# Depthwise convolution in the first mixer: taps behind the bonus products, one tile of channels on ScalarE and GpSimd, the other on VectorE

## The chip, the cores and the metric

The kernel runs on one core of a Trainium2 chip. The metric is the device time of one execution in microseconds; smaller is better. The engines of the core work in parallel, each on its own queue in the order of that queue: TensorE (PE) for matrix products, VectorE (DVE), ScalarE (ACT), GpSimd (POOL), and SyncE (SP), which issues the transfers.

## The reference, cut to what matters

Two blocks follow one another on 256 tokens of 1024 channels. The first has two layers; each is a gated feed-forward, a mixer and another feed-forward. The mixer projects the normalised input and gives its columns to three parts: a recurrence with six heads (RWKV), an attention with six heads and three dilations, and a convolution on 256 channels. The second block (one layer) isn't touched.

```python
def _conv_mixer(u, dw_w, dw_b, ln_w, ln_b):
    z = u[..., :D_CONV] * jax.nn.sigmoid(u[..., D_CONV:])        # D_CONV = 256
    z = lax.conv_general_dilated(z, dw_w[:, None, :], window_strides=(1,),
                                 padding=[(CONV_WIDTH - 1, 0)],   # CONV_WIDTH = 31
                                 dimension_numbers=('NWC', 'WIO', 'NWC'),
                                 feature_group_count=D_CONV) + dw_b
    mu = jnp.mean(z, axis=-1, keepdims=True)
    var = jnp.mean(jnp.square(z - mu), axis=-1, keepdims=True)
    z = (z - mu) * lax.rsqrt(var + CONV_LN_EPS) * ln_w + ln_b
    return jax.nn.silu(z)
...
    # first_block, layer l
    y_rwkv = _rwkv7_mixer(p_rwkv, ...)   # its last lines:
        # bonus = sum(rh * kh * r_k, axis=-1) * vh;  return (y + bonus) * g
    y_attn = _attention_mixer(...)
    y_conv = _conv_mixer(...)
    mix = jnp.concatenate([y_rwkv, y_attn, y_conv], axis=-1)
    x = x + mix @ w_out[l]
```

Each channel of the convolution is a sum of 31 products: the channel's row of 256 tokens, shifted by 0 to 30 tokens, times one weight, plus a bias.

## The kernel before

Activations lie with channels on the 128 partitions and the 256 tokens along the row. So the convolution's 256 channels are two tiles of 128x256, and a tap of one tile is one operation on 128x256 values with one weight per partition. All matrix products are in fp32 in two halves: ScalarE makes the upper half `whi` of each weight chunk `wraw` (L299), VectorE the rest `wlo` (L275), and TensorE multiplies with both.

The helpers record every operation under their own lines: L275 is `tt` (add, sub, mul), L288 `ts` (a tensor with one or two scalars), L294 `stt` (a tensor times a scalar per partition, plus or times a second tensor), L299 `act`, L302 `mm`, L306 `tr` (a transpose on TensorE). So in the profile operations are told apart by their tiles.

The tiles `Ea` and `Eb` are one scratch space, `E`, cut at element 6144: what is taken from `E` at a lower offset lies in `Ea`, the rest in `Eb`. `bigA`, `bigB` and `F` are further scratch spaces whose parts are used again for many things. The scheduler tracks waits by what overlaps there.

`mixer1` (L601 on) writes out one mixer. `project` makes the projection in pairs of tiles (`win`). `conv_in` projects the convolution's own four tiles and then, at raised priority (`first(PRI)`, PRI = 300), starts the generator `conv`: the gate `z` (in `Eb`), and the halved weights `wh` (tile `cwh`, one buffer for both layers). `rwkv` builds the recurrence's inputs, from the key norms `kks` through the bonus products `bon` (TensorE multiplies `rkb`, three tiles of r_k at `E(5632)`, with `r`). After `bon` come the triangular solves of its two streams, each with five doubling levels (`lt`, `l1` and a 32x32 transpose, L837), and then `z` and `u`. Between them it calls `taps()`, which carries the generator on over its 31 taps. Then `attn1` records the attention, whose scores get their biases from GpSimd (L288 and L275, 128x384, tile `F`) and whose maxima and sums VectorE takes (L1103, L1106), and then `mixer1` runs the end of `conv`: the mean by TensorE (`cm`), its subtraction (`Eb<-cm`), the square, the second mean, the scaling, silu, and the split for `w_out`. The first products with `w_out` (`woa`) take the convolution's two tiles, then the attention's; they fill TensorE between the recurrence's steps.

In a tap of before, ScalarE multiplies by the weight into `th` (128x256, one place per tile of channels) and GpSimd adds it to the sum `o`:

```python
for j in range(31):
    for i in range(2):
        a, w = z[:, i, j:j + TOK], wh[:, i * 31 + j:i * 31 + j + 1]
        if j == 0: self.act(o[:, i, :], a, AF.Identity, scale=w, bias=...)
        else:
            self.act(th[:, i, :], a, AF.Copy, scale=w)
            self.add(o[:, i, :], o[:, i, :], th[:, i, :], nc.gpsimd)
```

That is 62 ACTIVATEs and 60 adds in a layer. `z`, `th` and `o` all lie in `Eb`.

Each engine's order isn't that of the code. A list scheduler places the operations by priority, which falls in the order in which the code records them and is raised under `first`, and by estimated times; only what `pin` marks keeps its written order. So a call that moves, as `taps()` does, gives its operations another priority, and all four engines' orders around it are laid anew.

Of the kernel before, what the change touches and what calls it, by code (L numbers as in the profile page):

```python
# [15 lines left out]
AF = mybir.ActivationFunctionType  # L16
# [5 lines left out]
TOK = 256  # L22
# [192 lines left out]
class Ker:  # L215
# [385 lines left out]
    def mixer1(self, l, nxt):  # L601
# [57 lines left out]
        def conv_in():  # L659
            proj(10, 14)  # L660
            with self.first(PRI):
                next(conv)
        tail = self.rwkv(l, cb, col, lt, ps_sh, R1, R2, E, conv_in, lambda: next(conv))
        proj(14, len(order))
        with self.first(1000):
# [59 lines left out]
    def rwkv(self, l, cb, col, lt, ps_sh, R1, R2, E, between, taps):  # L725
        nc = self.nc
# [5 lines left out]
        th = E(5376, TOK)  # L732
# [83 lines left out]
        def stream(c_):  # L816
# [36 lines left out]
            if c_ == 0:  # L853
# [6 lines left out]
                for i in range(3):  # L860
                    ps = ring("bon")
                    self.mm(ps[:, 0:TOK], rkb[:, i, :], r[:, i, :], True, True)
                    self.mul(bv[:, i, :], ps[:, 0:TOK], v[:, i, :])
            if c_ == 0:
                taps()
            Tm = R2(3072 + c_ * 384, 384)
            for b in (2, 4, 8, 16, 32):

# [35 lines left out]
            if c_ == 0:  # L904

                for z in range(2):
                    ps = ring("bkt")
                    for i in range(3):
                        self.tr(ps[:, i * P:(i + 1) * P], BK[:, 2 * i, z, :])
                    self.act(BKt[:, z, :], ps[:, 0:384])  # L910
                for i in range(3):
                    ps = ring("lo2")
                    self.mm(ps[:, 0:TOK], lw[64:128, i * P:(i + 1) * P], th[64:128, :], True, True)

                    self.stt(bv[:, i, :], bv[:, i, :], col("rwkv_ln_b", i), ps[:, 0:TOK], ALU.add, ALU.mult)
                    self.act(g[:, i, :], ps[:, 0:TOK], AF.Copy, scale=col("rwkv_ln_w", i))

            psz = st["z", c_] = [ring("z0"), ring("z1")]
            for h in range(6):
# [12 lines left out]
        def tail(fill):  # L932
# [76 lines left out]
            gb(1, rw1, yc1)  # L1009

        stream(0)
        stream(1)
        for i in range(3):
            self.mixh[i] = (out[2 * i], out[2 * i + 1])
        return tail

    def conv(self, l, cb, col, cu, E):
        nc = self.nc
        W = 30 + TOK
        z = E(7168, 2, W)  # L1020
        nc.gpsimd.memset(z[:, :, 0:30], 0.0)
        th = E(7744, 2, TOK)
        self.act(th, cu[:, 2:4, :], AF.Tanh, scale=0.5)
        self.stt(z[:, :, 30:W], th, 1.0, cu[:, 0:2, :], ALU.add, ALU.mult)
        wh = self.t([P, 62], "cwh")
        self.ts(wh, col("conv_dw_w", 0, 62), 0.5, None)
        o = E(8256, 2, TOK)
        yield

        for j in range(31):  # L1030
            for i in range(2):
                a, w = z[:, i, j:j + TOK], wh[:, i * 31 + j:i * 31 + j + 1]
                if j == 0:
                    self.act(o[:, i, :], a, AF.Identity, scale=w, bias=col("conv_dw_b", i))
                else:
                    self.act(th[:, i, :], a, AF.Copy, scale=w)
                    self.add(o[:, i, :], o[:, i, :], th[:, i, :], nc.gpsimd)
        yield
        ps = self.pd("cm")
        for i in range(2):  # L1040
            self.mm(ps[:, 0:TOK], self.ones, o[:, i, :], i == 0, i == 1)
        for i in range(2):
            self.stt(o[:, i, :], ps[:, 0:TOK], -1.0 / 256, o[:, i, :])
        sq = E(7744, 2, TOK)
        self.act(sq, o, AF.Square)
        self.add(sq[:, 0, :], sq[:, 0, :], sq[:, 1, :])
        self.nacc = sq[:, 0, :]
        r = self.norm_cols(eps=1e-5, n=256.0, st="c", pool=self.pd)
        ps = self.pd("cb")
        for tt in range(2):  # L1050
            self.bcast_tok(ps[:, tt * P:(tt + 1) * P], r[:, tt:tt + 1])
        self.mul(o, o, ps[:, 0:TOK].unsqueeze(1).to_broadcast([P, 2, TOK]))
        for i in range(2):
            t1 = self.w1("ct1")
            self.ts(o[:, i, :], o[:, i, :], col("conv_ln_w", i), col("conv_ln_b", i))
            self.act(t1, o[:, i, :], AF.Tanh, scale=0.5)
            self.ts(t1, t1, 0.5, 0.5)
            self.mul(o[:, i, :], o[:, i, :], t1)
            self.mix_out(6 + i, o[:, i, :])
# [871 lines left out]
```

## Time and profile before

| | |
|---|---|
| median of 3 runs | 1712.67 us (1712.02 to 1713.77) |
| profiled execution | 1711.67 us |
| its span, first to last instruction | 1709.9 us |
| mean granted TensorE clock | 0.984 |
| mixer of layer 0, `kks` to `u` | 233.35 to 350.05 us |
| mixer of layer 1, `kks` to `u` | 787.28 to 895.68 us |
| TensorE, VectorE, ScalarE, GpSimd busy | 97%, 79%, 55%, 28% of the span |

The page's busy shares are means over the whole span. A mixer has other limits than the feed-forwards, so it is read by stretches. The views by window give, for a stretch, its length and each engine's busy time with the number of operations, then the granted clock of TensorE as a share of full speed and the transfers' share. The timeline gives single instructions with start and duration, and in brackets the engine's idle time just ahead of them and what ended it. Groups by form give a total and a mean in ns.

### The profile page before, as it was taken

The page shows a single profiled execution, that of the slowest core. Times are in us where ns is not written, and L with a number is a line of the kernel's source. Part 1 is how long each engine was busy: PE and PEld are TensorE (multiplying, and loading weights), DVE is VectorE, ACT ScalarE, POOL GpSimd, SP SyncE. Part 2 cuts the span into 40 slices and gives each one's busy share as a digit, 9 for nine tenths or more (in the row PEclk, how much of TensorE's full clock was granted, in tenths as well). Part 3 has the DMA queues.
Part 4 walks back from the last instruction along what each step waited for, and adds up shares of the span by engine and source line. Part 5 has one row for each costly group of instructions (what it writes and reads, how often), then busy time and mean ns, then how long its engine had stood idle before and what let it go on. Part 6 is the DMA issues. An engine that isn't in the chain of part 4 may idle for free.

```text
span 1709.9 us, 35224 instructions
## 1 busy us (share of the span) xinstructions
PE 1659.5 (97%) x14120; PEld 1567.6 (92%) x14120; DVE 1349.1 (79%) x2364; ACT 943.8 (55%) x1735; POOL 477.2 (28%) x429
## 2 busy tenths in 40 slices
PE   8999999999999999999999999999999999999997
PEld 8999997689999999999778999998988779999976
DVE  7886798568885788578967888787887867788877
ACT  5554476346454554457644555475657565566633
POOL 2221138212220122114921221063651140111142
PEclk9999998899999999999999999999999999999999
DMA  7775641027766687664102787644433226566533
GB/s 240 256 240 194 214 151 63 2 74 233 238 228 191 219 288 281 196 207 148 62 14 89 259 297 268 207 153 135 158 124 102 74 89 209 175 184 186 161 124 122
DMA packets 82132, 293.02 MB, mean 171 GB/s; under 512 B 9008, under 2 KB 10800, under 8 KB 81968
## 3 DMA queue, kind: packets, MB, share of 16 engines
q1 hardware_dynamic: 81968, 290.78, 52.0%
q8 instruction: 110, 1.80, 0.4%
q14 instruction: 54, 0.44, 0.1%
HBM read 289.69 MB, written 1.05 MB: 170 GB/s over the span
## 4 chain that ended last, share of the span: by engine, by line
PE 82%; DVE 10%; POOL 4%; ACT 2%; issue 2%; DMA 0%; SPq 0%; DVEq 0%; POOLq 0%; ACTq 0%
PE gu L302 35%; PE dn L302 17%; PE p L302 7%; PE win L302 5%; DVE wlo L275 3%; PE o L302 2%; POOL Eb L275 2%; PE woa L302 1%; DVE Eb L294 1%; PE ob L302 1%; DVE bigA L275 1%; PE s L302 1%; PE pt L306 1%; PE y L302 1%; ACT whi L299 1%
## 5 line engine op out<-in xcount | busy, mean ns | idle before, releaser
L299 ACT ACTIVATE whi<-wraw 128x1024 fp32r<-128x1024 f32 (+2 forms) x485 | 495.6, 1026 | 471.0 <-issue 132.8
L275 DVE TENSOR_TENSOR wlo<-wraw,whi 128x1024 fp32r<-128x1024 f32 (+2 forms) x477 | 574.7, 1205 | 173.7 <-ACT whi L299 170.6
L302 PE MATMUL gu<-xm,whi 128*128 128x256 f32 x2816 | 486.7, 278 | 6.1 <-ACT whi L299 4.0
L302 PEld LDWEIGHTS gu<-xm,whi 128*128 128x128 f32 x2816 | 428.1, 189 | 7.1 <-ACT whi L299 4.0
L302 PE MATMUL gu<-xm,wlo 128*128 128x256 f32 x1408 | 390.5, 278 | 2.8 <-DVE wlo L275 2.8
L302 PEld LDWEIGHTS gu<-xm,wlo 128*128 128x128 f32 x1408 | 265.4, 189 | 4.4 <-DVE wlo L275 4.3
L275 POOL TENSOR_TENSOR bigB<-Ea,bigA 128x256 fp32r<-128x256 f32 x88 | 123.5, 1406 | 421.0 <-ACT bigA L299 421.0
L302 PE MATMUL dn<-bigB,whi 128*128 128x256 f32 x704 | 194.1, 276 | 0.0
L302 PE MATMUL dn<-bigA,wlo 128*128 128x256 f32 x704 | 194.1, 276 | 0.0
L302 PE MATMUL dn<-bigA,whi 128*128 128x256 f32 x704 | 193.9, 276 | 0.0
L302 PE MATMUL p<-xm,whi 128*128 128x256 f32 x912 | 176.4, 288 | 1.9 <-DVE bigB L294 1.9
L302 PEld LDWEIGHTS p<-xm,whi 128*128 128x128 f32 x912 | 144.2, 191 | 8.4 <-issue 7.1
L302 PE MATMUL win<-xm,whi 128*128 128x256 f32 x736 | 136.1, 285 | 0.0
L302 PEld LDWEIGHTS dn<-bigB,whi 128*128 128x128 f32 x704 | 132.1, 188 | 0.0
L302 PEld LDWEIGHTS dn<-bigA,wlo 128*128 128x128 f32 x704 | 132.1, 188 | 0.0
L302 PEld LDWEIGHTS dn<-bigA,whi 128*128 128x128 f32 x704 | 132.0, 188 | 0.0
L275 POOL TENSOR_TENSOR Eb<-Eb 128x256 f32<-128x256 f32 x120 | 104.7, 900 | 96.2 <-ACT Eb L299 95.8
L302 PE MATMUL p<-xm,wlo 128*128 128x256 f32 x456 | 130.0, 285 | 0.0
L302 PE MATMUL gu<-bigA,whi 128*128 128x258 f32 x704 | 128.1, 284 | 0.0
L302 PEld LDWEIGHTS win<-xm,whi 128*128 128x128 f32 x736 | 114.4, 191 | 4.0 <-issue 4.0
L302 PEld LDWEIGHTS gu<-bigA,whi 128*128 128x128 f32 x704 | 109.7, 191 | 0.0
L302 PE MATMUL win<-xm,wlo 128*128 128x256 f32 x368 | 104.2, 284 | 0.0
(500 smaller groups left out, 3219.9 us busy)
## 6 DMA issues: line engine op xcount, KB each, us to landing
wraw<-in_wflat_dram SPq DMA_DIRECT2D x464, 512.0 KB, 3.6
Ea<-in_wmod_dram SPq DMA_DIRECT2D x24, 512.0 KB, 5.1
Eb<-in_wmod_dram SPq DMA_DIRECT2D x24, 512.0 KB, 4.6
F<-in_wflat_dram SPq DMA_DIRECT2D x22, 512.0 KB, 4.2
Ea<-in_cc_dram SPq DMA_DIRECT2D x6, 512.0 KB, 6.1
cb<-in_cb_dram SPq DMA_DIRECT2D x2, 608.0 KB, 4.7
Ea<-in_ctxT_dram SPq DMA_DIRECT2D x1, 1024.0 KB, 6.3
out_dram<-bigA SPq DMA_DIRECT2D x4, 256.0 KB, 2.2
```

Source lines behind the costliest of these rows:

```text
L275: (eng or self.nc.vector).tensor_tensor(out=out, in0=a, in1=b, op=op)
L294: self.nc.vector.scalar_tensor_tensor(out=out, in0=a, scalar=s, in1=b, op0=op0, op1=op1)
L299: self.nc.scalar.activation(out=out, in_=a, func=func, **kw)
L302: return self.nc.tensor.matmul(out, l, r, start=start, stop=stop, skip_group_check=True)
L306: self.nc.tensor.transpose(out, a, self.ident[0:n, 0:n])
```

## The change

Three things change, in both layers. `taps()` is called behind the solve of stream 0 instead of ahead of its doubling levels. The sum `o` moves from `E(8256)` to `E(5632)`, that is from `Eb` into `Ea`, onto the place of `rkb`, which the bonus products read; so no tap can be done before `bon`. And the taps of the second tile of channels (i = 1) become one VectorE operation each, 30 in a layer, multiplying and adding at once, with no ScalarE and GpSimd operation; those of the first tile stay a ScalarE product and a GpSimd add, 30 pairs in a layer, with two places for the product, used in turn. The first tap (j = 0) stays on ScalarE for both.

```diff
@@ -861,8 +861,6 @@
                     self.mul(bv[:, i, :], ps[:, 0:TOK], v[:, i, :])
-            if c_ == 0:
-                taps()
             Tm = R2(3072 + c_ * 384, 384)
             for b in (2, 4, 8, 16, 32):
@@ -914,6 +912,8 @@
                     self.act(g[:, i, :], ps[:, 0:TOK], AF.Copy, scale=col("rwkv_ln_w", i))
+            if c_ == 0:
+                taps()
 
             psz = st["z", c_] = [ring("z0"), ring("z1")]
@@ -1024,7 +1024,8 @@
-        o = E(8256, 2, TOK)
+
+        o = E(5632, 2, TOK)
         yield
@@ -1032,9 +1033,12 @@
                     self.act(o[:, i, :], a, AF.Identity, scale=w, bias=col("conv_dw_b", i))
+                elif i:
+                    self.stt(o[:, i, :], a, w, o[:, i, :])
                 else:
-                    self.act(th[:, i, :], a, AF.Copy, scale=w)
-                    self.add(o[:, i, :], o[:, i, :], th[:, i, :], nc.gpsimd)
+                    t = th[:, j % 2, :]
+                    self.act(t, a, AF.Copy, scale=w)
+                    self.add(o[:, i, :], o[:, i, :], t, nc.gpsimd)
```

Each engine's order differs from that of before only between `kks` and the first `u` of each mixer, and in two rows of small constants at the start.

GpSimd in layer 0, from the small operations that make the recurrence's inputs (`bigB<-bigB,bigA`) on; the adds of taps are `Eb<-Eb`, the attention's biases `F<-cb` and `F<-F,cb`. Before:

```order
L275 TENSOR_TENSOR Eb<-Eb 128x256 x14
L275 TENSOR_TENSOR bigB<-bigB,bigA 128x6x128
L275 TENSOR_TENSOR Eb<-Eb 128x256 x2
L275 TENSOR_TENSOR bigB<-bigB,bigA 128x768
L275 TENSOR_TENSOR Eb<-Eb 128x256 x34
L288 TENSOR_SCALAR F<-cb 128x384
L275 TENSOR_TENSOR Eb<-Eb 128x256
```

Now, with the adds as `Ea<-Ea,Eb`:

```order
L275 TENSOR_TENSOR bigB<-bigB,bigA 128x6x128
L275 TENSOR_TENSOR bigB<-bigB,bigA 128x768
L275 TENSOR_TENSOR Ea<-Ea,Eb 128x256 x2
L288 TENSOR_SCALAR F<-cb 128x384
L275 TENSOR_TENSOR Ea<-Ea,Eb 128x256
L288 TENSOR_SCALAR F<-cb 128x384
L275 TENSOR_TENSOR F<-F,cb 128x384
L275 TENSOR_TENSOR Ea<-Ea,Eb 128x256
L275 TENSOR_TENSOR F<-F,cb 128x384
L275 TENSOR_TENSOR Ea<-Ea,Eb 128x256 x10
```

Of the 50 adds ahead of the first bias two are left there; the other 28 of the now thirty stand between the biases and behind them.

VectorE in layer 0, in the middle of the solves and of the attention's second part (`bigA<-bigA,l...` and the transposes are levels of the solves; `xm<-aof,xm` and `F<-asc,nwt_ya,F` are the attention; `bigB<-lt,cb` belongs to the levels too). Before:

```order
L275 TENSOR_TENSOR bigA<-bigA,l_3218 128x6x16x2
L837 STREAM_TRANSPOSE bigB<-bigA 128x6x64
L288 TENSOR_SCALAR cwh<-cols 128x62
L275 TENSOR_TENSOR xm<-aof,xm 128x256
L294 SCALAR_TENSOR_TENSOR F<-asc,nwt_ya,F 128x128
L294 SCALAR_TENSOR_TENSOR F<-asc,nwt_ya,F 128x256
L275 TENSOR_TENSOR bigB<-lt,cb 128x192
```

Now:

```order
L294 SCALAR_TENSOR_TENSOR Ea<-Eb,cwh,Ea 128x256
L837 STREAM_TRANSPOSE bigB<-bigA 128x6x64
L294 SCALAR_TENSOR_TENSOR Ea<-Eb,cwh,Ea 128x256
L275 TENSOR_TENSOR bigB<-lt,cb 128x192
L294 SCALAR_TENSOR_TENSOR Ea<-Eb,cwh,Ea 128x256 x11
L294 SCALAR_TENSOR_TENSOR F<-asc,nwt_ya,F 128x128
L294 SCALAR_TENSOR_TENSOR F<-asc,nwt_ya,F 128x256
L294 SCALAR_TENSOR_TENSOR Ea<-Eb,cwh,Ea 128x256
L275 TENSOR_TENSOR xm<-aof,xm 128x256
```

The 30 taps stand singly and in runs, of which this is the longest; a later one has seven. The weights of the next layer, `cwh<-cols`, stood ahead of the attention's `xm<-aof,xm`; now they stand behind all of VectorE's taps.

TensorE in layer 0, ahead of the first `u` (`l_...` are the products `l1` of the levels, `tr`, `bkt`, `lo_...` and `z_...` the solve's end and what follows it). Now:

```order
L302 MATMUL lo_3262<-Ea,cb 128x256
L302 MATMUL woa<-xm,whi 128x256
L302 MATMUL woa<-xm,wlo 128x256
L302 MATMUL woa<-xm,whi 128x256
L302 MATMUL woa<-xm,wlo 128x256
L302 MATMUL woa<-xm,whi 128x256 x2
L302 MATMUL woa<-xm,wlo 128x256
L302 MATMUL woa<-xm,whi 128x256 x2
L302 MATMUL woa<-xm,wlo 128x256
L302 MATMUL l_3576<-bigB 64x64 x4
```

The first product with `w_out`, which reads the convolution's result, stands ahead of the last `l1` here, and so of `z` and `u`, which come behind that.

## Rows read from the trace of the kernel before

**Rows 1.** The page: span, busy share of each engine, shares of the last chain.

```profile
span 1709.9 us, 35224 instructions
PE 1659.5 (97%) x14120; PEld 1567.6 (92%) x14120; DVE 1349.1 (79%) x2364; ACT 943.8 (55%) x1735; POOL 477.2 (28%) x429
...
PE 82%; DVE 10%; POOL 4%; ACT 2%; issue 2%; DMA 0%; SPq 0%; DVEq 0%; POOLq 0%; ACTq 0%
```

**Rows 2.** Windows, layer 0: `kks` to `bon`, the bonus, B, C, behind `u`.

```profile
core 0: us, PE busy (x) PEld busy (x) DVE busy (x) ACT busy (x) POOL busy (x), PEclk, DMA share, GB/s
233.35:287.63 54.28, 51.62 (x351) 46.40 (x352) 48.97 (x83) 37.57 (x74) 43.52 (x47) 0.94 0.32 98
287.63:291.80 4.17, 2.57 (x12) 1.12 (x10) 4.12 (x8) 3.76 (x10) 3.29 (x4) 0.90 0.00 0
291.80:309.68 17.88, 15.53 (x187) 11.22 (x187) 12.05 (x38) 10.22 (x30) 16.10 (x20) 0.79 0.08 30
309.68:350.05 40.37, 38.13 (x504) 29.72 (x501) 22.55 (x73) 15.46 (x40) 2.27 (x4) 0.89 0.05 15
350.05:387.12 37.07, 33.87 (x332) 31.70 (x331) 25.25 (x70) 17.15 (x39) 6.71 (x6) 1.00 0.28 85
```

**Rows 3.** Windows, layer 1: `kks` to `bon`, B, C, behind `u`.

```profile
787.28:843.68 56.40, 52.01 (x381) 46.33 (x380) 52.50 (x83) 40.94 (x82) 47.09 (x50) 0.97 0.31 94
...
845.45:870.56 25.11, 23.55 (x385) 17.51 (x385) 19.25 (x60) 12.70 (x38) 16.61 (x20) 0.96 0.07 23
870.56:895.68 25.12, 24.01 (x284) 19.55 (x281) 15.11 (x49) 11.77 (x29) 0.83 (x2) 0.93 0.01 2
895.68:933.09 37.41, 34.11 (x330) 31.80 (x329) 25.25 (x70) 17.48 (x40) 6.71 (x6) 1.00 0.32 97
```

**Rows 4.** Timeline, TensorE: start, duration, operation [idle ahead, what ended it].

```profile
266.13 1.20 PE L302 MATMUL sc<-bigB,Ea 64*128 64x256 f32 x4 [1.32 <-DVE bigA L275]
...
289.38 0.70 PE L302 MATMUL bon<-bigB,Ea 128*128 128x256 f32 x2 [0.94 <-ACT Ea L299]
290.75 1.06 PE L302 MATMUL bon<-bigB,Ea 128*128 128x256 f32 x2 [0.67 <-DVE Ea L275]
...
841.90 0.44 PE L306 MATMUL avt<-cm,Eb 128*128 128x128 f32 x2 [2.02 <-DVE Eb L275]
```

**Rows 5.** GpSimd: a timeline row of layer 0; groups by form, layer 1.

```profile
265.60 8.76 POOL L275 TENSOR_TENSOR Eb<-Eb 128x256 f32<-128x256 f32 x12 [0.68 <-ACT Eb L299]
...
L275 POOL TENSOR_TENSOR Eb<-Eb 128x256 f32<-128x256 f32 x60 | 53.0, 910 | 47.6 <-ACT Eb L299 47.4
L288 POOL TENSOR_SCALAR F<-cb 128x384 f32<-128x384 f32 x4 | 4.9, 1214 | 1.6 <-DVE F L294 1.6
...
L275 POOL TENSOR_TENSOR F<-F,cb 128x384 f32<-128x384 f32 x4 | 4.0, 1000 | 0.0
```

**Rows 6.** VectorE beside GpSimd (timeline), and operations with `cwh` (least/median/most ns).

```profile
269.60 0.67 DVE L402 TENSOR_SCALAR nwt_ya<-nwt_ia 128x24 int32<-128x24 int32 x1
...
272.85 0.17 DVE L275 TENSOR_TENSOR nwt_ta<-nwt_ya 128x24 f32<-128x24 f32 x1
...
1205.60 0.96 DVE L294 SCALAR_TENSOR_TENSOR Eb<-F,Eb 128x256 f32<-128x256 f32 x1
1206.48 0.47 DVE L294 SCALAR_TENSOR_TENSOR Eb<-F,cwh,Eb 128x256 f32<-128x256 f32 x1
...
L299 ACT ACTIVATE Eb<-Eb,cwh x120: 491/508/534, 237.8 to 861.5; 128x256 f32<-128x256 f32 x120
...
L294 DVE SCALAR_TENSOR_TENSOR Eb<-F,cwh,Eb x12: 386/474/695, 1172.7 to 1219.0; 128x256 f32<-128x256 f32 x12
```

**Rows 7.** Timeline: `cwh` in layer 0; `cm` subtraction and first `u`, layer 1.

```profile
304.84 0.20 DVE L288 TENSOR_SCALAR cwh<-cols 128x62 f32<-128x62 f32 x1 [5.62 <-ACT Eb L299]
...
870.56 0.75 DVE L294 SCALAR_TENSOR_TENSOR Eb<-cm,Eb 128x256 f32<-128x256 f32 x2
...
895.68 1.51 PE L302 MATMUL u<-bigB,bigA 128*128 128x64 f32 x9
```

## The prediction, made before the result

> **What bounds the kernel now.** The page comes first [rows 1]: TensorE is busy 97% of the span and the chain of work that ended last lies on it for 82%. So a change to other engines' work can matter only where TensorE stands still, runs at its lower clock, or passes small products back and forth with VectorE. The order of instructions says where to look: before and after, each engine's order is the same except between the key-norm products `kks` and the first `u` of the two mixers (and two rows of small constants at the start). Everything behind `u` keeps its order and its 37.1 us (37.4 in the second layer) [rows 2, 3]. So the prediction is a sum over two stretches: 233.35 to 350.05 us and 787.28 to 895.68 us.
>
> The busy time by stretch [rows 2, 3] divides each in three. **Stretch A**, up to the bonus products `bon`, is the input projection: TensorE is busy 51.62 of 54.28 us and 52.01 of 56.40 us, at mean clocks of 0.94 and 0.97. All but about a dozen of the 60 tap pairs run here today, on ScalarE and GpSimd. **Stretch B**, from the bonus to the mean's subtraction of the convolution (`Eb<-cm`), holds the first levels of the triangular solves and most of the attention. TensorE is nominally busy there with products of 64 columns, each waiting for VectorE's last result; VectorE is busy 12.05 of 17.88 us in layer 0 and 19.25 of 25.11 us in layer 1. **Stretch C**, from there to `u`, took 40.37 us in layer 0, where the solves came last, and 25.12 us in layer 1, where the end of the convolution, the first products with `w_out` and `u` follow one another [rows 3, 7].
>
> **The change part by part.** *Taken away from A.* The taps' ACTIVATEs (about 0.51 us) and adds leave A altogether, because the new place of the sum overlaps `rkb`, which `bon` reads. What they do to others there is visible. VectorE's small operations on 12 or 24 elements take 0.67 us while GpSimd adds taps back to back, and 0.17 us when they miss one [rows 5, 6]; 0.73 us is one add (8.76 / 12). So VectorE loses time to GpSimd's adds, and TensorE then waits for VectorE: 1.32 us for `sc`, 2.02 us for `avt`, and 0.94 and 0.67 us at the bonus itself, the first of these for ScalarE [rows 4].
>
> Of A, then, layer 0 gives back its idle 54.28 - 51.62 = 2.66 us and the bonus' 4.17 - 2.57 = 1.60 us; layer 1 gives back 56.40 - 52.01 = 4.39 us. The low clock costs up to 6% of 54.28 = 3.3 us and 3% of 56.40 = 1.7 us. The 64-row `sc` and two-column `as` products ahead of its fall are still there, so I take half: 1.6 and 0.8 us. Gain: **5.9 us in layer 0, 5.2 us in layer 1**. Bounds: nothing, if other waits take their place, and 7.6 and 6.1 us.
>
> *Added to B.* Thirty multiply-adds per layer on VectorE (128x256, two SBUF sources) and, at the same time, thirty adds on GpSimd and thirty ACTIVATEs on ScalarE. ScalarE is busy 12.70 of 25.11 us in layer 1's B, and its 30 x 0.51 us are hidden beside GpSimd's adds. GpSimd has 30 x 0.73 = 21.9 us, plus the attention's four biases of 1.21 + 1.00 us, 8.8 us: 30.7 us alone. At today's mean of 0.91 us (53.0 / 60, with its own waits for VectorE) it is 36 us [rows 5]. VectorE has its 19.25 us and thirty taps. What is one tap worth? Alone, the same operation with the same kind of operands takes 0.47 us. Beside a GpSimd operation it takes up to 0.695 us, and its neighbour `Eb<-F,Eb` takes 0.96 us when a GpSimd add has just begun [rows 6]. In the new order 18 of layer 0's 30 taps stand in two runs, of 11 and 7, where nothing else separates them and GpSimd has ten and thirteen adds in a row; there each tap meets one add. The other 12 stand between reductions, transposes and PSUM reads. I take 0.70 us for the mean, nearest to the row of the same operation; bounds 0.47 and 0.96. So B becomes 19.25 + 30 x 0.70 = **40.3 us** (33.4 to 48.1) in either layer, VectorE being never idle in it. GpSimd's 36 us end a little before.
>
> The Trainium skill (SBUF — State Buffer, "SBUF: two separate sides") says that VectorE with two SBUF inputs and GpSimd take an exclusive lock for the whole instruction and the loser fully blocks; the rule speaks against putting the two halves side by side. By it a pair would cost 0.73 + 0.47 = 1.20 us; the 0.96 us above shows the blocking, but with a part of the instruction beside it.
>
> *What comes last then.* C in layer 1 is already what follows the convolution's end: subtraction, square, sum, reciprocal root, scaling, `w_out`, `z`, `u`. In the new order the first `w_out` product stands ahead of the last solve level and `z` on TensorE in both layers, so whoever waits for the convolution holds up `u`. I keep its 25.1 us for both.
>
> Layer 1: 40.3 - 25.1 = +15.2, less 5.2: **+10.0 us**. Layer 0: B and C were 350.05 - 291.80 = 58.2 us and become 40.3 + 25.1 = 65.4: +7.2, less 5.9: **+1.3 us**. Layer 0 loses less because it has an old stall in B: VectorE stands 5.62 us at the next layer's weights `cwh`, which wait for ScalarE's last tap [rows 7]. That instruction now stands behind VectorE's own 30 taps, where GpSimd and ScalarE are nearly done, so it should wait little (up to 4 us, were GpSimd at 44 instead of 36 us; then the solves behind it wait too). Behind it are queued the attention's reductions and the levels 16 and 32 of the solves. SP's queue isn't touched: no DMA is moved, and the weight chunks of these stretches come as before.
>
> Sum: +11.3 us. The profiled execution took 1711.67 us (span 1709.9); it would become 1723.0. The median of the runs is 1.0 us above it: **1724.0 us**.
>
> **The rivals.** *Faster: a tap is hidden at its bare price.* The taps would find GpSimd delayed (its later adds wait for ScalarE, which waits for VectorE's reductions), or slip in between its adds. At 0.47 us B is 33.4 us: layer 1 +8.3 - 6.1, layer 0 +0.3 - 7.6: -5.1 us, 1707.6 us, with all of A's gain. For it: VectorE is idle 5.86 us in layer 1's B today, and half the GpSimd work leaves the program. Against it: these idle times lie between dependent steps, and the taps are themselves one chain. The sum is zero at 0.70 - 11.3 / 60 = 0.51 us for a tap; below that this rival wins.
>
> *Same.* Taps of 0.46 to 0.57 us with the likely gain of A: within 3.4 us of 1713; layer 0 wins what layer 1 loses.
>
> *Slower still: strict turns in the runs.* Every tap meets an add: 0.96 us, B 48.1 us, and only the idle time of A comes back: layer 1 +23.0 - 4.4, layer 0 +15.0 - 4.3: +29 us, 1742 us. For it: GpSimd and VectorE both run dependent chains, and each release hands the turn to the other. Against it: 12 taps stand singly.
>
> *The whole lock.* 1.20 us for each pair makes B 55.3 us: layer 1 +30.2 - 5.2, layer 0 +22.2 - 5.9: +41 us, 1754 us. The 0.96 us row speaks against it. This is the mechanism of the Trainium skill's sentence on the lock; the trace agrees only with a lock for part of the instruction.
>
> **How the numbers follow.** About 0.2%, 3.4 us, is what a measurement of this kernel can tell from no change. Chances: the forecast 0.51 (its own range 1717 to 1735, taps of 0.58 to 0.88 us), strict turns 0.09, whole lock 0.04: slower 0.64. Same 0.15. Faster 0.21. The range reaches from 1706 us, just under the faster rival, to 1736 us; left out are the larger part of strict turns, the whole lock, and the case that B needs less than VectorE's own sum.
>
> **What would show it.** Right: TensorE's idle time ahead of `bon` near 1 us, and VectorE's 12-element operations at 0.17 us there; `bon` some 5 us earlier after `kks`; then VectorE busy over 95% from `bon` to `Ea<-cm`, taps of 0.5 to 1.0 us, near 0.7 in the mean; that stretch near 40 us in both layers; `u` 1 us later after `kks` in layer 0 and 10 us in layer 1; everything behind `u` unchanged. Wrong: taps of 0.5 us in the mean; a B under 34 us; TensorE waiting as long ahead of `bon` as now; or a first `w_out` product that doesn't wait for the convolution.

## The result and the profile after

The changed kernel took 1732.68 us (median of 4 runs, 1727.29 to 1735.46) against 1712.47 us: a ratio of 1.0113, with a 95% interval of 1.0084 to 1.0142. It is slower, as forecast, by 20.2 us where 11.3 were forecast. The profiled execution took 1730.2 us. Ratios here and below leave out two executions far above the rest, one of the kernel before (2341 us) and one of psum_sum (7919 us). The page, to be read beside [rows 1]:

```profile
span 1728.4 us, 35231 instructions
PE 1672.5 (97%) x14120; PEld 1576.2 (91%) x14120; DVE 1366.8 (79%) x2424; ACT 918.4 (53%) x1675; POOL 422.6 (24%) x369
...
PE 83%; DVE 10%; issue 2%; ACT 2%; POOL 2%; DMA 0%; POOLq 0%; SPq 0%; DVEq 0%; ACTq 0%
```

TensorE is busy 13 us longer, with the same 14120 products, VectorE 18 us longer with 60 operations more; GpSimd has 60 operations and 55 us less. The mean granted clock went from 0.984 to 0.976.

The same stretches as in [rows 2, 3], by windows: first the two from `kks` to the end of `bon`, then B and C of layer 0, then B and C of layer 1.

```profile
core 0: us, PE busy (x) PEld busy (x) DVE busy (x) ACT busy (x) POOL busy (x), PEclk, DMA share, GB/s
232.94:288.45 55.51, 55.31 (x396) 48.81 (x396) 44.88 (x94) 20.04 (x35) 4.81 (x3) 0.94 0.31 97
789.87:847.86 57.99, 57.56 (x372) 49.33 (x372) 43.83 (x87) 19.97 (x35) 5.35 (x4) 0.91 0.31 96
...
288.45:331.70 43.25, 33.30 (x394) 24.26 (x395) 41.33 (x97) 23.53 (x62) 32.72 (x37) 0.68 0.03 12
331.70:352.76 21.06, 21.06 (x265) 17.62 (x264) 12.09 (x38) 10.62 (x25) 0.82 (x2) 1.00 0.01 2
...
847.86:889.04 41.18, 31.50 (x401) 22.95 (x401) 39.35 (x93) 21.94 (x58) 31.59 (x37) 0.75 0.04 14
889.04:915.39 26.35, 23.58 (x277) 19.61 (x272) 13.94 (x46) 11.79 (x29) 0.83 (x2) 0.94 0.04 5
```

From `kks` to `u` layer 0 takes 119.8 us (116.9 before) and layer 1 125.5 us (108.6): 3.0 and 17.0 us more. Here and below `kks` is the start of its first product, 233.19 and 787.12 us in the kernel before, 0.16 us ahead of the 233.35 and 787.28 of [rows 2, 3]. Between the first `u` of layer 0 and the `kks` of layer 1 lie 437.1 us in both kernels. Outside the two stretches only 1.4 us were gained (1.2 of them behind the second `u`), so that the profiled executions are 18.5 us apart and not 20.

Two things are to be seen. Up to the bonus TensorE now stands still for only 0.2 and 0.4 us (4.3 and 4.4 before), yet it comes out 3.1 us sooner in layer 0 and 0.3 us in layer 1. And in B VectorE is busy 96% of the time, where it was 67% and 77% [rows 2, 3].

VectorE's timeline in layer 0 shows what a tap costs: a run of eleven, a single one, another single one, a run of seven.

```profile
292.41 0.46 DVE L294 SCALAR_TENSOR_TENSOR Ea<-Eb,cwh,Ea 128x256 f32<-128x256 f32 x1
...
298.56 7.95 DVE L294 SCALAR_TENSOR_TENSOR Ea<-Eb,cwh,Ea 128x256 f32<-128x256 f32 x11
...
314.21 0.88 DVE L294 SCALAR_TENSOR_TENSOR Ea<-Eb,cwh,Ea 128x256 f32<-128x256 f32 x1
...
318.17 5.65 DVE L294 SCALAR_TENSOR_TENSOR Ea<-Eb,cwh,Ea 128x256 f32<-128x256 f32 x7
```

0.46 us is a tap that meets no add, 0.88 one that does; the runs give 0.72 and 0.81 us for each. The mean over 30 is 0.73 us in layer 0 and 0.69 in layer 1. GpSimd's timeline, beside the first run and beside the second:

```profile
300.02 5.16 POOL L275 TENSOR_TENSOR Ea<-Ea,Eb 128x256 f32<-128x256 f32 x6 [1.07 <-ACT Eb L299]
...
314.77 11.31 POOL L275 TENSOR_TENSOR Ea<-Ea,Eb 128x256 f32<-128x256 f32 x13
```

The second row is a pace of 0.87 us for an add, where the row of [rows 5] has 0.73. The eleven taps of the first run met these six adds and the end of one before them; then GpSimd had nothing to add until 308.9 us. So 0.72 us is a mean of taps that met an add and taps that met none.

### The profile page after: what moved, and what is told of

The parts are those of the page before. It is cut to its first block, busy times and chain, and to the rows that moved or that the text cites. A ratio compares the mean times of both kernels' runs of the same rounds, so it can differ in the third digit from the quotient of the medians.

```text
span 1728.4 us, 35231 instructions
## 1 busy us (share of the span) xinstructions
PE 1672.5 (97%) x14120; PEld 1576.2 (91%) x14120; DVE 1366.8 (79%) x2424; ACT 918.4 (53%) x1675; POOL 422.6 (24%) x369
## 4 chain that ended last, share of the span: by engine, by line
PE 83%; DVE 10%; issue 2%; ACT 2%; POOL 2%; DMA 0%; POOLq 0%; SPq 0%; DVEq 0%; ACTq 0%
PE gu L302 34%; PE dn L302 16%; PE win L302 7%; PE p L302 7%; DVE wlo L275 3%; PE o L302 2%; PE sc L302 2%; PE woa L302 1%; DVE Ea L294 1%; PE ob L302 1%; DVE Eb L294 1%; PE s L302 1%; PE pt L306 1%; PE y L302 1%; PE c L302 1%
## 5 line engine op out<-in xcount | busy, mean ns | idle before, releaser
L275 DVE TENSOR_TENSOR wlo<-wraw,whi 128x1024 fp32r<-128x1024 f32 (+2 forms) x477 | 567.6, 1191 | 173.8 <-ACT whi L299 170.5
L302 PE MATMUL gu<-bigA,wlo 128*128 128x258 f32 x352 | 99.8, 284 | 0.0
```

The costliest lines, as they stand in the source:

```text
L275: (eng or self.nc.vector).tensor_tensor(out=out, in0=a, in1=b, op=op)
L302: return self.nc.tensor.matmul(out, l, r, start=start, stop=stop, skip_group_check=True)
```

## The experiments

No run was made for the place of the call alone, but one of the mixed placings below tells. In mixed the call stands at its new place and the first tile's sum at its old one, and that tile's products begin at 238.3 us, as they do in the kernel before (237.8 [rows 6]). So what moves the taps behind `bon` is the sum's new place on `rkb`, not the call.

**The changed kernel again** (label after_again), no edit.

> The changed kernel once more, unaltered, for a second profiled execution beside the first (1730.2 us). My theory: the stretch from the key norms to the end of the bonus products is bound by TensorE there, and its length follows the stretches at half clock that fall into it: 55.5 us in layer 0 with 3.4 us lost to the clock, 58.0 us in layer 1 with 5.1 us lost. Where this execution loses more or less there, the stretch is longer or shorter by the same amount, within 1 us; and the stretch from the bonus to the mean's subtraction stays at 43 and 41 us, within 2 us. Rival: the length is set by waits, and stays the same whatever the clock does.

1729.21 us (4 runs, ratio 1.0103, 1.0088 to 1.0118). By windows, `kks` to the end of `bon` in either layer, then B in either layer:

```profile
233.72:286.12 52.40, 52.20 (x396) 46.27 (x396) 44.90 (x94) 20.06 (x35) 4.82 (x3) 1.00 0.35 104
787.56:843.97 56.41, 56.00 (x372) 48.45 (x372) 43.71 (x87) 19.98 (x35) 5.34 (x4) 0.94 0.31 95
...
286.12:329.12 43.00, 28.65 (x397) 20.73 (x398) 41.42 (x97) 23.28 (x62) 31.85 (x37) 0.81 0.03 11
843.97:885.17 41.20, 30.43 (x401) 22.04 (x401) 39.41 (x94) 22.00 (x58) 31.61 (x37) 0.79 0.04 13
```

The same 396 products took 52.40 us at a clock of 1.00 and 55.51 us at 0.94. Other kernels below have this stretch's order on TensorE too, but for a product or two at its end, which makes a table (times without a name are the changed kernel's two executions):

| layer | clock 1.00 | clock 0.94 | clock 0.91 |
|---|---|---|---|
| 0 | 52.40, 52.41 (move_only), 52.44 (no_pool), 52.43 (pool_single) | 55.51, 55.51 (both_dve), 55.54 (no_taps) | |
| 1 | 53.39 (no_pool), 53.26 (pool_single), 53.39 (no_taps) | 56.41, 56.38 (both_dve) | 57.99, 57.97 (move_only) |

The stretch's length is told by the clock to 0.2 us. B is the other way round: 43.25 us at a clock of 0.68 and 43.00 at 0.81, 41.18 at 0.75 and 41.20 at 0.79. There the clock costs nothing: VectorE is busy 96% of it.

**The split alone** (split_old): before's place of sum and call, the changed kernel's taps.

```diff
+                elif i:
+                    self.stt(o[:, i, :], a, w, o[:, i, :])
                 else:
-                    self.act(th[:, i, :], a, AF.Copy, scale=w)
-                    self.add(o[:, i, :], o[:, i, :], th[:, i, :], nc.gpsimd)
+                    t = th[:, j % 2, :]
+                    self.act(t, a, AF.Copy, scale=w)
+                    self.add(o[:, i, :], o[:, i, :], t, nc.gpsimd)
```

> The split alone: one tile of channels as 30 VectorE multiply-adds, the other as 30 pairs on ScalarE and GpSimd, with the sum and the call where they were before. In this kernel's order 25 to 29 of VectorE's taps stand ahead of the bonus products. My theory: VectorE is the one to be late there, since it is busy 46 of 51 to 54 us without any taps: 46.4 + 27 x 0.60 = 63 us up to the bonus instead of 54 and 56, so 8 us lost in each layer; in layer 0 the stall at the next layer's weights goes (taps end earlier), which gives back some 8 us behind the bonus: 1712 + 16 - 8 = about 1720 us. Rival: with half of GpSimd's adds gone VectorE's other work is quicker and the taps fill its idle time: 1705 us. Second rival: the split is what costs, wherever it stands: 1732 us as in the changed kernel.

1757.10 us (1.0271, 1.0255 to 1.0286), the slowest of all. `kks` to the end of `bon` by windows:

```profile
232.82:306.64 73.82, 64.33 (x346) 54.36 (x344) 62.41 (x109) 32.23 (x61) 35.13 (x32) 0.75 0.25 79
804.71:878.81 74.10, 65.32 (x346) 55.13 (x344) 62.31 (x105) 32.26 (x62) 36.18 (x32) 0.72 0.27 85
```

And TensorE's longest waits there in layer 0 (total us, times, longest):

```profile
PEld sc L302 <- POOL Eb L275: 7.4, 1, 7.4
PE sc L302 <- DVE Ea L294: 7.2, 1, 7.2
```

VectorE has 62 us of work there, as I expected (63), but the stretch takes 74. TensorE's wait of 7 us comes ahead of `sc`, and the mean clock of the stretch is 0.75 and 0.72, as if half of it ran at the lower level. So being late on VectorE was seen; the size was short, by the wait and the low clock together, which no run parts. The 8 us that layer 0 was to get back behind the bonus did not come: to `u` it took 56.4 us (58.2 before), and layer 1 lost there, 60.5 us for 50.2.

**The move alone** (move_only): the sum on `rkb` and the moved call, the taps as before (60 pairs).

```diff
-                elif i:
-                    self.stt(o[:, i, :], a, w, o[:, i, :])
                 else:
-                    t = th[:, j % 2, :]
-                    self.act(t, a, AF.Copy, scale=w)
-                    self.add(o[:, i, :], o[:, i, :], t, nc.gpsimd)
+                    self.act(th[:, i, :], a, AF.Copy, scale=w)
+                    self.add(o[:, i, :], o[:, i, :], th[:, i, :], nc.gpsimd)
```

> The move alone: the sum lies where the changed kernel puts it, so that no tap is done before the bonus products, but all 60 taps of a layer are pairs of ScalarE and GpSimd as before. My theory: GpSimd sets the stretch from the bonus to the mean's subtraction, with 60 adds of 0.80 us and 8.8 us of biases: 57 us instead of 43 and 41 in the changed kernel, so 14 and 16 us more: 1732 + 30 = about 1762 us; the stretch up to the bonus as in the changed kernel. Rival: VectorE, which no longer takes taps, lets GpSimd run at its bare 0.73 us and the adds of layer 1 are hidden in part: 1750 us. Were the split the costly part of the change, this one would be faster than the changed kernel.

1737.69 us (1.0155, 1.0139 to 1.0170). B and C by windows:

```profile
286.67:344.21 57.54, 50.12 (x611) 37.97 (x611) 25.16 (x77) 43.19 (x109) 51.50 (x69) 0.73 0.03 10
344.21:359.24 15.03, 8.70 (x45) 8.13 (x44) 7.04 (x26) 2.83 (x7) 0.00 (x0) 0.55 0.00 0
...
854.23:908.97 54.74, 40.01 (x559) 29.82 (x560) 26.44 (x76) 39.87 (x102) 50.66 (x68) 0.78 0.03 11
908.97:925.75 16.78, 16.78 (x120) 15.33 (x121) 8.13 (x29) 6.31 (x15) 0.41 (x1) 0.69 0.00 1
```

B is 57.5 us, as worked out (57), and 54.7. But the kernel is only 8 us above the changed one, not 30: C is 15.0 and 16.8 us in place of 21 to 27, because most of the solves had been done during B: in layer 0 TensorE has 45 products left in C, where the changed kernel has 265. C is no constant. It holds the convolution's end and whatever of the solves is still to do, and what B takes longer C may take less.

**GpSimd's taps left out** (no_pool): the first tile's 30 pairs aren't computed.

```diff
                 elif i:
                     self.stt(o[:, i, :], a, w, o[:, i, :])
-                else:
-                    t = th[:, j % 2, :]
-                    self.act(t, a, AF.Copy, scale=w)
-                    self.add(o[:, i, :], o[:, i, :], t, nc.gpsimd)
```

> The changed kernel with the 30 pairs of the first tile of channels left out (only its first tap is computed), so that no GpSimd add stands beside VectorE's 30 taps. My theory: each tap costs 0.47 us of its own and the rest of its 0.73 and 0.69 us is waiting for GpSimd's adds. Then the taps take 0.47 to 0.52 us, and the stretch from the bonus to the mean's subtraction goes from 43 and 41 us to 19 + 30 x 0.49 = 34 us: 16 us less, about 1717 us. Rival: the taps are one chain in which each waits for the last one's end, and cost 0.70 us whoever is beside them: no change to that stretch, 1732 us.

1711.78 us (10 runs, 1.0000, 0.9982 to 1.0018). The group of VectorE's taps, with the least, the median and the most of one in ns:

```profile
L294 DVE SCALAR_TENSOR_TENSOR Ea<-Eb,cwh,Ea x60: 434/484/1044, 288.1 to 859.7; 128x256 f32<-128x256 f32 x60
```

B by windows, layer 0 and layer 1:

```profile
285.91:317.94 32.03, 25.91 (x387) 19.11 (x386) 30.90 (x93) 9.64 (x32) 9.20 (x8) 0.84 0.05 17
833.12:866.47 33.35, 23.99 (x361) 17.52 (x362) 31.66 (x93) 10.34 (x34) 9.26 (x8) 0.90 0.04 16
```

A tap takes 0.49 and 0.51 us in the mean of the two layers, B 32.0 and 33.4 us. So some 0.2 us of each tap in the changed kernel came from the pairs beside it (pool_single below keeps their ScalarE half and shows that it was GpSimd's add), and the chain of taps by itself costs no more than its bare price.

**The sum in PSUM** (psum_sum): VectorE's sum lies in PSUM up to the last tap; the taps are recorded after the projection, since only then is a PSUM buffer free.

```diff
-        tail = self.rwkv(l, cb, col, lt, ps_sh, R1, R2, E, conv_in, lambda: next(conv))
+        tail = self.rwkv(l, cb, col, lt, ps_sh, R1, R2, E, conv_in, lambda: None)
         proj(14, len(order))
+        next(conv)
...
+        ps = self.pd("ctap")[:, 0:TOK]
...
                 elif i:
-                    self.stt(o[:, i, :], a, w, o[:, i, :])
+                    self.stt(o[:, i, :] if j == 30 else ps, a, w, ps)
```

> The changed kernel with one difference in what VectorE reads: the running sum of its tile of channels lies in PSUM until the last tap, so that a tap has one SBUF input (the shifted row) and one from PSUM; GpSimd's 30 adds stay beside it. In this order 8 to 10 of the 30 taps stand ahead of the last bonus product. My theory: the 0.21 us that a tap costs above its bare 0.49 us is VectorE waiting for GpSimd because both read two SBUF inputs. Then these taps take 0.42 to 0.50 us beside GpSimd's adds, the stretch from the bonus to the mean's subtraction takes 31 to 35 us instead of 43 and 41, and the kernel 1729 - 16 = about 1713 us (1709 to 1718). Rival: what is shared is not the inputs but the time slots of the two engines; the taps stay at 0.70 us and the kernel at 1729 us.

1718.40 us (10 runs, 1.0029, 1.0004 to 1.0053). The group of taps, as above:

```profile
L294 DVE SCALAR_TENSOR_TENSOR ctap<-Eb,cwh,ctap x58: 447/480/490, 277.1 to 861.7; 128x256 f32<-128x256 f32 x58
```

B by windows, layer 0 and layer 1:

```profile
289.52:328.50 38.98, 30.27 (x410) 22.47 (x410) 33.37 (x93) 22.72 (x60) 29.11 (x37) 0.78 0.05 15
842.29:879.52 37.23, 27.94 (x407) 20.63 (x408) 31.74 (x90) 21.90 (x59) 28.11 (x35) 0.88 0.03 11
```

No tap takes over 0.49 us, with GpSimd's 30 adds beside it. B is shorter by 4 us in either layer, where 6 to 12 were expected: in layer 0 VectorE is busy 33.4 of 39.0 us and no longer the bound; its taps end at 313 us, GpSimd's adds at 321.6, and the mean's products on TensorE stand behind products of the attention and the solves until 325. Seven of layer 0's taps lie ahead of this B. The kernel is 11 us faster than the changed kernel, and still not faster than before.

**GpSimd with one SBUF input** (pool_single): its add becomes the product times one, written over the sum, so the first tile's sum is left out.

```diff
-                    self.add(o[:, i, :], o[:, i, :], t, nc.gpsimd)
+                    self.ts(o[:, i, :], t, 1.0, None, eng=nc.gpsimd)
```

> The changed kernel with GpSimd's 30 adds turned into operations with one SBUF input (the product times one, written over the sum, so the first tile's sum is only its last product). VectorE's taps keep their two SBUF inputs. If the clash needs two SBUF inputs on both sides, VectorE's taps fall from 0.70 to 0.49 us and the stretch from the bonus to the mean's subtraction to 34 to 37 us; if any GpSimd operation on SBUF holds VectorE up, taps stay near 0.70 us and the stretch near 42 us. I give the first 0.6.

1719.60 us (one run). The group of VectorE's taps:

```profile
L294 DVE SCALAR_TENSOR_TENSOR Ea<-Eb,cwh,Ea x60: 434/484/1020, 288.8 to 872.7; 128x256 f32<-128x256 f32 x60
```

GpSimd's operations in layer 1, by form:

```profile
L288 POOL TENSOR_SCALAR Ea<-Eb 128x256 f32<-128x256 f32 x30 | 28.4, 948 | 33.7 <-ACT Ea L299 30.3 <-ACT Eb L299 1.7
```

The taps fall to 0.50 and 0.53 us in the mean: the clash of taps and adds comes from two SBUF inputs on both engines. The few taps of layer 1 that still take 0.90 to 1.02 us stand beside the attention's biases `F<-F,cb`, which have two inputs. This doesn't hold for every operation of VectorE: the TENSOR_SCALAR of [rows 6], 24 elements with one SBUF input, took 0.67 us beside the adds and takes 0.18 in the changed kernel, with no adds there. B stays at 42.2 and 42.8 us. This GpSimd operation comes every 0.94 us even behind the last tap (layer 0, nine in 8.50 us), and GpSimd ends at 327.4 us, the taps at 315.3: GpSimd is the bound. I had the taps right and B wrong.

**Both tiles on VectorE** (both_dve): the pairs become VectorE taps too.

```diff
-                elif i:
-                    self.stt(o[:, i, :], a, w, o[:, i, :])
                 else:
-                    t = th[:, j % 2, :]
-                    self.act(t, a, AF.Copy, scale=w)
-                    self.add(o[:, i, :], o[:, i, :], t, nc.gpsimd)
+                    self.stt(o[:, i, :], a, w, o[:, i, :])
```

> The changed kernel with both tiles of channels on VectorE: 60 taps of it in a layer, none on ScalarE and GpSimd (GpSimd keeps the attention's eight biases). My theory: a tap costs 0.49 us when no GpSimd add is beside it, so the stretch from the bonus to the mean's subtraction is 19.3 + 60 x 0.49 = 49 us instead of 43 and 41. What follows gets shorter, since the solves go on meanwhile: in the kernel with all taps on GpSimd a longer stretch (57.5 and 54.7 us) left 15.0 and 16.8 us behind it instead of 21 to 27. So bonus to the first u is 67 to 70 us instead of 64.4 and 68: 1729 + 3 to 8 = 1732 to 1737 us. Rival: without any clash the two tiles' taps, which are independent chains, alternate and cost less than one chain (0.42 us): 45 us and 1727 us.

1737.62 us (1.0138, 1.0102 to 1.0175), at the upper end of the 1732 to 1737 expected; bonus to `u` took 73.3 and 66.8 us, where 67 to 70 were expected. B by windows, layer 0 and layer 1:

```profile
288.84:339.17 50.33, 33.32 (x504) 25.05 (x504) 45.28 (x134) 12.58 (x39) 8.77 (x8) 0.83 0.03 11
855.60:905.68 50.08, 35.28 (x508) 26.48 (x510) 45.84 (x135) 12.33 (x38) 9.57 (x8) 0.80 0.03 11
```

B is 50 us (49 expected), with taps of 0.49 us. The price of a tap carries from one split to another.

**The weights of the next layer out of the queue** (before_cwhE): the kernel before, with the halved weights in unused scratch space.

```diff
-        wh = self.t([P, 62], "cwh")
+        wh = E(8768, 62)
```

> The kernel before with one difference: the halved weights of the taps lie in 62 unused elements of the scratch space instead of a tile of one buffer, so that the next layer's weights no longer stand in VectorE's queue behind ScalarE's last tap. VectorE's order is otherwise that of before. My theory, as in the prediction: layer 0 loses less by the change because the stall of 5.62 us in it goes; without it layer 0 from the bonus to u comes near layer 1's 50.2 us from its 58.2, so this kernel takes 1712 - 5 to 8 = about 1705 us, and layer 1 doesn't change. Rival: VectorE has slack there and the solves wait for TensorE's low clock or for the convolution anyway: 1711 to 1712 us.

1712.28 us (12 runs, 0.9998, 0.9973 to 1.0023): no change. VectorE's timeline where the stall of [rows 7] was:

```profile
306.57 0.77 DVE L275 TENSOR_TENSOR xm<-aof,xm 128x256 fp32r<-128x256 f32 x1 [5.91 <-ACT xm L299]
```

ScalarE's timeline ahead of it, one of the late taps, the last tap and the attention's result:

```profile
303.00 0.51 ACT L299 ACTIVATE Eb<-Eb 128x256 f32<-128x256 f32 x1 [0.76 <-POOL Eb L275]
...
305.73 0.51 ACT L299 ACTIVATE Eb<-Eb 128x256 f32<-128x256 f32 x1
306.14 0.40 ACT L299 ACTIVATE xm<-aof 128x256 fp32r<-128x256 f32 x1
```

The stall is 5.91 us now, one place further down the queue. The attention's result waits for ScalarE too, and ScalarE has it behind its last tap. What held VectorE up was ScalarE's queue of taps, and these waited in turn for GpSimd's adds, with one place for the product of each tile; the weights only stood first in line. As the stall moved and didn't go, this run doesn't show what it costs.

**No taps at all** (no_taps): only the first tap of each tile is computed.

```diff
-                elif i:
-                    ...
-                else:
-                    ...
```

> The changed kernel with all taps but the first two left out, on all engines. It gives the floor under any placing of the taps. My theory: up to the bonus 52.4 and 53.3 us, and 3 to 5 us more for each fall of the clock, as in every kernel whose taps come later; behind it what VectorE and the solves need by themselves, 22 us + 22 us, so 97 us for a mixer against 117 and 109 before: about 1680 us. Rival: the solves' chain between TensorE and VectorE is the bound there, and takes 50 us without any tap: 1692 us.

1696.60 us (one run). Bonus to `u` by windows:

```profile
288.73:336.64 47.91, 44.40 (x653) 34.47 (x652) 31.14 (x106) 21.19 (x58) 9.87 (x10) 1.00 0.05 14
827.74:881.03 53.29, 48.42 (x675) 37.61 (x675) 33.45 (x107) 21.27 (x59) 9.42 (x10) 0.90 0.07 21
```

47.9 and 53.3 us with no tap, near the rival's 50 and not the 44 that I took, though VectorE has only 31 and 33 us of work. In layer 0 the chain that ended last passes between TensorE and VectorE (products of the solves and the attention, reductions, transposes) up to 322 us and lies on TensorE alone behind that. The 5.4 us between the layers are those of the clock (53.29 x 0.10 = 5.3). Before, with most taps hidden ahead of the bonus, this took 58.2 and 50.2 us: layer 1, at a clock of 0.95, was shorter with its taps. By this one run all taps together cost the kernel before about 15 us (1711.52 in the same series). That is some measure of what another placing could bring; that none can bring more is not shown, since another order, or another clock, changes the floor too.

**Two mixed placings** (mixed, mixed2). In mixed the first tile's pairs begin early, as before, and VectorE's taps of the second come behind the bonus, where no add is left; in mixed2 ten taps of the second tile go to the early pairs as well (`elif i and j > 10`). The edit of mixed, in part:

```diff
-        o = E(5632, 2, TOK)
+        o = E(8256, 2, TOK)
+        late = E(5632, TOK)
...
-                    self.act(o[:, i, :], a, AF.Identity, scale=w, ...)
+                    self.act(late if i else o[:, i, :], a, AF.Identity, scale=w, ...)
                 elif i:
-                    self.stt(o[:, i, :], a, w, o[:, i, :])
+                    self.stt(o[:, i, :] if j == 30 else late, a, w, late)
```

> Both prices avoided in turn: the first tile's 30 pairs on ScalarE and GpSimd begin as early as in the kernel before (all of them stand ahead of the bonus products in this order), and VectorE's 30 taps of the second tile come behind the bonus, where no GpSimd add is left. My theory: a VectorE tap costs 0.49 us there, so bonus to u takes 56 to 57 us, as in the kernel without GpSimd's taps (56.5 and 56.9), against 58.2 and 50.2 before; up to the bonus, half the adds cost half of what TensorE stood idle, so 54 us and 55 us without a fall of the clock, 3 to 5 us more with one. Sum 1706 to 1713 us, 1709 as the middle. Rival: the adds that are left hold VectorE up as much as all did, and the clock falls in both layers: 1716 us.

> The same with 40 pairs in a layer ahead of the bonus (all of the first tile and ten of the second) and 20 VectorE taps behind it. My theory: up to the bonus as before, 55 to 58 us with the clock's falls; the stretch from the bonus to the mean's subtraction 19.3 + 20 x 0.49 = 29 us, and with 21 to 25 us behind it bonus to u takes 50 to 54 us in both layers against 58.2 and 50.2: layer 0 gains 4 to 8 us, layer 1 loses 0 to 4: 1705 to 1712 us. Rival: the gain in layer 0 is not there, because the solves come last in it whoever does the taps: 1713 us.

mixed 1723.66 us (11 runs, 1.0066, 1.0043 to 1.0090), mixed2 1719.98 us (11 runs, 1.0038, 1.0019 to 1.0057): neither beats the kernel before. mixed by windows, up to the end of `bon`, then to `u`:

```profile
234.23:293.79 59.56, 57.99 (x393) 50.49 (x391) 50.43 (x94) 32.71 (x63) 34.18 (x32) 0.91 0.30 91
786.87:841.55 54.68, 53.02 (x393) 46.72 (x391) 50.08 (x89) 33.15 (x63) 34.55 (x32) 1.00 0.34 104
293.79:349.85 56.06, 47.21 (x654) 36.46 (x655) 43.29 (x133) 20.40 (x57) 10.41 (x10) 0.91 0.03 10
841.55:899.56 58.01, 48.68 (x655) 37.65 (x655) 45.00 (x135) 20.40 (x57) 10.28 (x10) 0.91 0.03 9
```

In the profiled execution the stretches are near what was expected: behind the bonus 56.1 and 58.0 us (56 to 57), ahead of it 54.7 without a fall of the clock (55) and 59.6 with one (57 to 59). It took 1715.76 us at a clock of 0.986. But the 11 runs go with their clock from 1713.93 us at 0.985 to 1730.86 at 0.974, and seven of them have 0.979 or less. So the terms were about right and the clock wrong; where it fell in the other ten is not on record. mixed2 has 54.6 and 55.5 us behind the bonus (50 to 54 expected) and 57.0 and 63.8 us ahead of it, at clocks of 0.94 and 0.87.

## Why the prediction came out as it did

The way and the range were right, the size was short: 1724.0 us against 1732.7 and, in the second series, 1729.2. Term by term, for the profiled execution and the second one:

| term | forecast | first | second |
|---|---|---|---|
| layer 0: `kks` to the end of `bon` | -5.9 | -3.1 | -6.2 |
| layer 1: the same | -5.2 | -0.3 | -1.9 |
| a tap, mean of layer 0 and of layer 1 | 0.70 | 0.73, 0.69 | 0.70, 0.69 |
| B, layer 0 and layer 1 | 40.3 | 43.3, 41.2 | 43.0, 41.2 |
| C, layer 0 and layer 1 | 25.1 | 21.1, 26.4 | 21.4, 27.5 |
| layer 0 in all | +1.3 | +3.0 | 0.0 |
| layer 1 in all | +10.0 | +17.0 | +16.6 |

**The step that was mis-sized is the gain in A.** It gave back TensorE's idle time and half of what the low clock cost. The idle time did come back: TensorE stood still 0.2 and 0.4 us. The small operations are quick again, too. One group of them by form in layer 0 of the kernel before (three operations; total us, mean ns):

```profile
L275 DVE TENSOR_TENSOR nwt_tr<-nwt_yr 128x12 f32<-128x12 f32 x3 | 2.1, 699 | 0.0
```

The same group in the changed kernel:

```profile
L275 DVE TENSOR_TENSOR nwt_tr<-nwt_yr 128x12 f32<-128x12 f32 x3 | 0.5, 168 | 0.1
```

But the clock did not halve its loss. The length of the stretch times what its clock lacks to 1.00 gives 3.3 and 5.2 us in the first execution, 0 and 3.4 in the second, where the sum had left 1.6 and 0.9. Why it falls in one execution and not in the next stays open. With it at 1.00 the stretches take 52.4 and 53.3 us, which is 6.2 and 5.0 us less than before and what was forecast (52.7 and 53.1); the first profiled execution had 0.94 and 0.91, the second 1.00 and 0.94. In the first this term alone misses 7.7 us, a little more than the 7.2 us by which the sum missed its 1730.2; the rest nearly cancels. In the second, with a miss of 6.2 us, 3.0 us net are here and 3.3 us in layer 1's B and C, where C ran at 0.88.

**The price of a tap, 0.70 us, held**, and so did its reason: 0.49 us without GpSimd's adds (no_pool), 0.48 beside them with one input in PSUM (psum_sum). One step to it didn't: not every tap of the two runs met an add, since GpSimd had six and a part for the eleven. So that the mean came out so near is in part luck. The faster rival, which wanted the bare price, fell; so did strict turns and the whole lock. The Trainium skill's sentence on the lock (SBUF — State Buffer, "SBUF: two separate sides") has the loser block for the whole instruction. By the rows of [rows 5, 6] that is an estimated 1.20 us a pair, and the trace disagrees: in the run of seven a tap and an add together took 0.87. There they do take turns, as the rival of strict turns has it, but not in the other taps, and a pair costs less than its 0.96.

**B followed from it** within 1 to 3 us, and VectorE was busy 96% of it, as said. It wasn't the only bound: the chain that ended last lies on VectorE's taps for 47% of B in layer 0, but in layer 1 on GpSimd's adds and biases for 34%.

**C was right in size and wrong in kind.** It was taken to be the convolution's end alone, and so constant. In layer 1 of the changed kernel the first `w_out` product did wait for the convolution:

```profile
902.99 0.38 PE L302 MATMUL woa<-xm,whi 128*128 128x256 f32 x1 [0.84 <-ACT xm L299]
```

In layer 0 TensorE had no idle time ahead of it. VectorE's timeline there, with the convolution's last step:

```profile
343.79 0.76 DVE L275 TENSOR_TENSOR xm<-Ea,xm 128x256 fp32r<-128x256 f32 x2 [0.30 <-ACT xm L299]
```

TensorE's, with the first `w_out` product and the first `u`:

```profile
344.04 0.38 PE L302 MATMUL woa<-xm,whi 128*128 128x256 f32 x1
...
352.76 0.44 PE L302 MATMUL u<-bigB,bigA 128*128 128x64 f32 x3
```

TensorE is busy for all 21.06 us of that C, at a clock of 1.00, with the last levels of the solves, `z` and the `w_out` products: it is TensorE's own work, and VectorE has only 12.09 us there. move_only, where most of the solves lie in B, has 15 us for C. So C would have shrunk had B been longer. That the fixed 25.1 us did no harm here (bonus to `u`: 65.4 forecast, 64.3 and 67.5 measured) is luck of the size.

**The stall at `cwh` was named after the wrong cause.** It did go in the changed kernel (the instruction waits for nothing), and layer 0 did lose less than layer 1. But before_cwhE shows that the weights had no part in it. ScalarE's taps had, which waited for GpSimd: half of them are gone in the changed kernel, and the product has two places. Why layer 0 was 8 us longer than layer 1 behind the bonus before is only partly known: the clock there was 0.86 against 0.95 (58.24 x 0.14 - 50.22 x 0.05 = 5.6 us of low clock more), and no run separated that from the stall.

Of the change's two parts, each alone is worse than both: the split at the old place costs 45 us, the move alone 26, both together 17 to 20. At the new place the split is worth 8 us, since VectorE takes half of GpSimd's 60 adds; at the old one it puts 17 us on an engine that has 44 to 45 us to do in a stretch that TensorE could leave after 52 to 53.

## What to carry to other kernels

Before work is moved off an engine that is only in the way, ask for the floor of the place it goes to: here VectorE had 31 to 33 us of work in 48 to 53 us, much of it steps between which TensorE works, and 30 operations of 0.49 us were not hidden there. Price VectorE and GpSimd together where both read two SBUF inputs (0.70 us here for 0.49 alone); one input in PSUM ended it for these taps. And a stall on an instruction says which engine is waited for, not that this instruction is the cause: look for the next one in the queue that waits for the same engine, and for what that engine waits for.

## What the runs showed of the hardware that was not expected

- The same instructions in the same order took 52.4, 55.5 or, in layer 1, 53.3, 56.4 or 58.0 us from one execution to the next, by the granted clock of the stretch alone (1.00, 0.94, 0.91, a mean of stretches at 2.4 and at 1.2 GHz). What TensorE did before the falls (64-row `sc` products, then the two-column `as`) was the same where there was none. The runs of one kernel spread accordingly: 1713.9 to 1730.9 us for mixed.
- Where VectorE was busy 96% of the stretch, a clock of 0.68 in place of 0.81 cost nothing (43.25 and 43.00 us).
- Taking one SBUF input from either side nearly ended the clash of taps and adds: GpSimd with one SBUF input (0.92 to 0.95 us each in the mean) left VectorE's two-input taps at 0.50 to 0.53 us, and VectorE with one SBUF input and one from PSUM kept 0.48 us beside GpSimd's two-input adds. What is left falls on GpSimd's operation: 0.95 us in the mean of nine beside taps (pool_single, from 308.9 us), 0.87 in that of the nine behind the last tap.
